# The end of a decoder step: the last output tile's first 256 columns in two products with sums of their own

## The chip, the cores and the metric

The program runs on one core of one Trainium2 chip, as one launch. The metric is device time in microseconds (us). Before the change three runs gave 953.62, 954.85 and 957.12 us; the median is 954.85 us.

## The reference, cut to what matters

One trunk layer of a decoder for 512 prompt tokens and 8 x 8 sample tokens, 1024 channels wide, all in float32. The change lies in its last two operations: the down-projection of the feed-forward part with its gated residual add, and the final RMSNorm.

```python
def _rmsnorm(x, g):
    x32 = x.astype(jnp.float32)
    y = x32 * lax.rsqrt(jnp.mean(x32 * x32, axis=-1, keepdims=True) + RMS_EPS)
    return (y * g.astype(jnp.float32)).astype(x.dtype)
...
    x = x + g2 * ((jax.nn.gelu(ac, approximate=False) * val) @ w_down)
...
    y_prompt = _rmsnorm(xp, final_g)
    y_sample = _rmsnorm(xs, final_g)
```

Every token's output needs the mean of the squares of all its 1024 channels, so no row of a token can be written before the last channel tile of that token is known.

## The kernel before, in words

Activations lie transposed: channels on the 128 partitions, tokens along the free axis. `x1` is a list of NK = 8 channel tiles of 128 x 576: columns 0 to 511 are the prompt tokens, columns 512 to 575 the sample tokens. `GRP = [(0, 256), (256, 576)]` cuts the columns into group 0 and group 1. At the very end the columns are seen as token tiles of 128 (`tok_cols`, L891): tile 0 is columns 0 to 127, tile 1 columns 128 to 255, tiles 2 and 3 the rest of the prompt, and tile 4 columns 448 to 575, of which only the 64 sample tokens are used.

A float32 product is made of three products of a faster form: each operand is split into a high and a low part (`fh`, `fl` for activations, `wh`, `wl` for weights), and high x high, low x high and high x low are added up in PSUM. The down-projection has 22 contraction tiles. Tiles 16 to 21 are the last stretch, and there the channel tiles 6 and 7 (`LATE = 2`) are made last, plainly: for a channel tile and a column group, 6 contraction tiles x 3 products = 18 matmuls into one PSUM bank (`down_late`, L2303, by `product_g`, L231). The weight part is the stationary operand, the activations move.

After such a product come, in this order:

- `residual` (L1640): VectorE reads PSUM, multiplies with the gate and adds to `x1[m]`.
- `summed` (L2211): ScalarE squares the result into `sq`; VectorE adds it to the sum of squares `acc3`, except for the very last piece, whose `sq` is kept apart; then ScalarE multiplies `x1[m]` in place with the gains of the final norm.
- `final_rows` (L2223): TensorE adds up squares over the channels, by a matmul with a 128 x 2 tile of ones (`acc3`, and for the last piece `sq` too), so that each token of a tile gets its sum on its own partition. `rows_rsqrt` (L624) scales it on VectorE and raises it to the power -1/2 on GpSimd, into a column of `r3`.
- `TokenTile` (L1809): `turn` transposes the eight channel tiles of one token tile by TensorE into two PSUM banks (a matmul with `ident`); `finish` reads both banks, multiplies each row with its factor in `r3` and writes `yo`, one bank by ScalarE and one by VectorE, and starts a store of each half.

PSUM has two pools here: `mmps()` gives one of two 128 x 1024 tiles (two banks each), `aux()` one of four banks.

Before the change the end runs so. Product of tile 6, group 0. Product of tile 7, group 0, of which four of six contraction tiles are made, 12 matmuls; then, between them (`between`), the row factors of tiles 2, 3 and 4 and the transposes and stores of tiles 2 and 3; then the other 6 matmuls. Then tile 4, then the row factors of tiles 0 and 1 in one go, then tiles 0 and 1. In tile 4, VectorE reads one bank and ScalarE the other. Stores go out on SyncE's queue, but for the two of tile 1, which ScalarE issues.

From `pinned.extend([pe, act, dve])` (L2313) on, the instructions of TensorE, ScalarE and VectorE stay in the order in which the program writes them. Each engine takes its own in that order, so an instruction that waits holds up all that are written behind it on its engine.

Of the kernel before, what the change touches and what calls it, by code (L numbers as in the profile page):

```python
# [12 lines left out]
AF = mybir.ActivationFunctionType  # L13
ALU = mybir.AluOpType
AX = mybir.AxisListType

P = 128
D = 1024
NK = D // P
# [3 lines left out]
GRP = [(0, 256), (256, 576)]  # L23
# [8 lines left out]
LATE = 2  # L32
# [44 lines left out]
def step_kernel(ctx: ExitStack, tc: tile.TileContext, ins: dict, outs: list):  # L77
    nc = tc.nc
# [14 lines left out]
    def nm(s):  # L93
        cnt[0] += 1
        return f"{s}{cnt[0]}"
# [37 lines left out]
    def sv(t):  # L133
        return t[:, 512:576]
# [474 lines left out]
    ones = cp.tile([P, 2], F32, tag="ones", name="ones")  # L609
# [302 lines left out]
    for i in (3, 4):  # L912
        a = aux()
# [24 lines left out]
    def queries(t, ps=None, scale=HD**-0.5):  # L938
# [50 lines left out]
        out=sel,  # L989
        in0=snk.rearrange("p (h g) -> p h g", h=4),  # L990
# [247 lines left out]
    def b10(t):  # L1238
        return t[:, 514:594].rearrange("p (b e) -> p b e", b=8)
# [184 lines left out]
    ya, w_next, raw_ao, o, late = [], {}, {}, [], []  # L1424
# [56 lines left out]
    for at, m in enumerate(PLAIN):  # L1481
        if at in (4, 5):
            src, dst = ((ins["cache_k_win"], nks), (ins["cache_v_win"], nvs))[at - 4]
# [39 lines left out]
        if at == len(PLAIN) - 1:  # L1523
# [5 lines left out]
        ps = product(w, h, steps)  # L1529
# [3 lines left out]
            out=b10(u)[:, :, 2:10], in0=b8(sv(ps)), in1=b8(sv(c_sb)), op=ALU.mult  # L1533
# [67 lines left out]
    for n, m in enumerate(turn):  # L1601
# [6 lines left out]
        ps = product(w_next.pop(n), o)  # L1608
# [31 lines left out]
    def residual(ps, xt, blk, c0=0, c1=NT, tail=dve):  # L1640

        p1 = min(c1, 512)
        dve.scalar_tensor_tensor(
            out=xt[:, c0:p1], in0=ps[:, : p1 - c0], scalar=modT[:, blk, 0:1], in1=xt[:, c0:p1],
            op0=ALU.mult, op1=ALU.add,
        )
        if c1 > 512:
            t = sp.tile([P, 64], F32, tag="rt", name=nm("rt"))
            tail.tensor_tensor(
                out=b8(t), in0=b8(ps[:, p1 - c0 :]), in1=bc(modT[:, blk, 1:9]), op=ALU.mult  # L1650
            )
            tail.tensor_tensor(out=sv(xt), in0=sv(xt), in1=t, op=ALU.add)
# [19 lines left out]
    x1 = [x1t[k // 4][:, k % 4, :] for k in range(NK)]  # L1672
# [20 lines left out]
    late = []  # L1693
# [115 lines left out]
    class TokenTile:  # L1809
# [14 lines left out]
        def finish(self, queues):  # L1824
            r, i = self.rows, self.i
            out = [slot("yo", shape=[P, 512]) for _ in range(2)]
            fr = r3[r, i : i + 1]
            a, d = (1, 0) if i == 4 else (0, 1)
            act.activation(out[a][r], self.ps[a][r], AF.Copy, scale=fr)
            dve.tensor_scalar(  # L1830
                out=out[d][r], in0=self.ps[d][r], scalar1=fr, scalar2=None, op0=ALU.mult
            )
            for hh, queue in enumerate(queues):
                cs = slice(hh * 512, hh * 512 + 512)
                dst = y_p[0, i * P : i * P + P, cs] if i < 4 else y_s.flatten_outer_dims()[:, cs]
                queue.dma_start(dst, out[hh][r])
# [309 lines left out]
    for k0, m in CHUNKS.items():  # L2146
        r = lambda *x, k0=k0: raw_op(k0, *x)
# [31 lines left out]
    for n, at in enumerate(order):  # L2179
# [7 lines left out]
        if n + 2 < len(order):  # L2187
            kind, m = order[n + 2]
# [7 lines left out]
        else:  # L2196
            summed = n + 1 in prepared
# [10 lines left out]
    acc3 = slot("acc")  # L2208
    r3 = cp.tile([P, 8], F32, tag="r3", name="r3")

    def summed(m, c0=0, c1=NT, last=False):  # L2211

        sq = acc3 if m == 0 else slot("sq")
        act.activation(sq[:, c0:c1], x1[m][:, c0:c1], AF.Square)
        if m and not last:
            dve.tensor_tensor(
                out=acc3[:, c0:c1], in0=acc3[:, c0:c1], in1=sq[:, c0:c1], op=ALU.add
            )
        x = x1[m][:, c0:c1]
        act.activation(x, x, AF.Copy, scale=par2T[:, 66 + m : 67 + m])  # L2220
        return sq

    def final_rows(g, sq=None):  # L2223

        a = mmps()
        i0, i1, step = (0, 2, 512) if g == 0 else (2, 5, 2)
        parts = [acc3] if sq is None else [acc3, sq]
        for n, x in enumerate(parts):
            for i in range(i0, i1):
                dst = a[:, (i - i0) * step : (i - i0) * step + 2]  # L2230
                matmul(dst, tok_cols(x, i), ones, start=n == 0, stop=n == len(parts) - 1)
        src = a[:, : (i1 - i0) * step].rearrange("p (i e) -> p i e", e=step)[:, :, 0]
        rows_rsqrt(r3[:, i0:i1], src)

    late, jobs, weight_steps = [], {}, {}
# [39 lines left out]
    fa = [fs.pop(m) for m in range(PLAIN_AT, LAST_AT)]  # L2275
# [24 lines left out]
        summed(m)  # L2300
    fa = [fs[m] for m in range(LAST_AT, NF)]

    def down_late(m, g, between=None):  # L2303
        ps = product_g(late[m - NK + LATE], fa, g, None if (m, g) == (NK - 1, 1) else mmps(), between)
        residual(ps, x1[m], 40 + m, *GRP[g])
        return summed(m, *GRP[g], last=(m, g) == (NK - 1, 0))

    for m in range(NK - LATE, NK):
        down_late(m, 1)
    down_late(NK - LATE, 0)  # L2310
    for m in range(NK - LATE + 1, NK - 1):
        down_late(m, 0)
    pinned.extend([pe, act, dve])  # L2313

    def others():
        final_rows(1)
        for i in (2, 3):
            tt = TokenTile(i)
# [12 lines left out]


_TC = {"schedule_with_timeline_sim": True}
# [31 lines left out]
```

## Time and profile before

| what | value |
|---|---|
| median of three runs | 954.85 us |
| the profiled execution's own time | 955.27 us |
| its span, first to last instruction | 953.5 us |
| mean granted TensorE clock | 0.996 |
| TensorE busy (matmul records) | 936.5 us, 98% of the span |
| VectorE, ScalarE, GpSimd busy | 739.7, 600.5, 199.8 us |
| last matmul record ends | about 946.3 us into the span |

The profiled execution's own time is 1.77 us longer than its span. A row of the timeline gives the start in the span, the time from the first start to the last end of the merged instructions, the engine, the source line, the operation, output and input by the program's names, the shape and the count; in brackets the idle time before it and who ended it. `PE` is TensorE, `PEld` its weight loads, `DVE` VectorE, `ACT` ScalarE, `POOL` GpSimd, `SPq` and `ACTq` the issue of DMAs by SyncE and ScalarE. Most operations here go through one recording helper, so all of them carry line 116 and are told apart by the names of their tiles.

### The profile page before, as it was taken

Reading aid. Unit: us, or ns where it says so; the run is one execution under the profiler, and the core shown is the slowest. Engines: PE = TensorE matmul, PEld = TensorE weight load, DVE = VectorE, ACT = ScalarE, POOL = GpSimd, SP = SyncE. Lnnn points to the kernel's source line nnn. Section 1 sums busy time; section 2 is a strip of 40 time slices with the busy share of each in tenths; the row PEclk is TensorE's granted clock in tenths of the full one; section 3 lists DMA queues with packets and bytes.
Section 4 is the critical chain, followed back from the end, with each engine's and each line's share of the span. In section 5 each row is a group of like instructions: output and inputs, shape, how many; then the busy total and the mean of one; then the engine's idle time right before and its main releaser. Section 6 shows DMA issues by size and latency. Waiting matters only on the chain. (4 is left out here: it accounts for less than half of the span.)

```text
span 953.5 us, 19148 instructions
## 1 busy us (share of the span) xinstructions
PE 936.5 (98%) x7227; PEld 901.4 (95%) x7227; DVE 739.7 (78%) x1395; ACT 600.5 (63%) x1158; POOL 199.8 (21%) x426
## 2 busy tenths in 40 slices
PE   7999999999999999999999999999999999999996
PEld 5799999898999989999889999999999999999996
DVE  4788988875866767876677688888888889877965
ACT  5474768656665446875335567577766776677574
POOL 2222120101111011210001231122243233421131
PEclk9999999999999999999999999999999999999998
DMA  9984233516545768899884832368679877986643
GB/s 281 329 252 109 70 101 98 157 70 151 141 130 171 248 217 214 213 248 291 278 289 122 184 102 67 96 137 198 164 153 233 207 169 167 228 211 151 143 97 105
DMA packets 190032, 166.74 MB, mean 175 GB/s; under 512 B 9177, under 2 KB 162973, under 8 KB 189651
## 3 DMA queue, kind: packets, MB, share of 16 engines
q1 hardware_dynamic: 172210, 114.41, 40.3%
q0 software_dynamic: 17440, 50.58, 24.8%
q8 instruction: 57, 0.93, 0.4%
q10 hardware_dynamic: 288, 0.52, 0.1%
q14 instruction: 37, 0.30, 0.1%
HBM read 116.84 MB, written 15.02 MB: 138 GB/s over the span
## 5 line engine op out<-in xcount | busy, mean ns | idle before, releaser
L116 ACT ACTIVATE whi<-raw 128x1024 fp32r<-128x1024 f32 (+3 forms) x198 | 195.4, 996 | 35.7 <-DVE raw L116 18.0
L116 DVE TENSOR_TENSOR wlo<-raw,whi 128x1024 fp32r<-128x1024 f32 (+3 forms) x153 | 176.1, 1156 | 33.9 <-ACT whi L116 33.4
L116 POOL DMA_DIRECT2D wlo<-raw x45 | 39.0, 866 | 207.2 <-PE mm L116 96.2
L116 DVE TENSOR_TENSOR raw<-raw 128x512 f32<-128x512 f32 (+1 forms) x104 | 69.2, 665 | 3.4
L116 PE MATMUL aux<-2h,whi 128*128 128x288 f32 (+2 forms) x232 | 63.5, 294 | 0.0
L116 PE MATMUL aux<-2l,whi 128*128 128x288 f32 (+2 forms) x232 | 63.5, 295 | 0.0
L116 PE MATMUL mm<-hh,whi 128*128 128x256 f32 (+2 forms) x264 | 60.4, 304 | 0.5 <-ACT hh L116 0.5
L116 PE MATMUL mm<-hl,whi 128*128 128x256 f32 (+2 forms) x264 | 57.3, 297 | 0.0
L116 PE MATMUL mm<-hh,wlo 128*128 128x256 f32 (+2 forms) x264 | 55.4, 295 | 0.0
L116 PE MATMUL aux<-hl,whi 128*128 128x288 f32 (+1 forms) x196 | 53.3, 298 | 0.0
L116 PE MATMUL aux<-hh,whi 128*128 128x288 f32 (+1 forms) x196 | 53.2, 297 | 0.0
L116 POOL DMA_DIRECT2D wl<-s x41 | 35.6, 867 | 71.4 <-ACT wl L116 53.6
L116 ACT ACTIVATE mm<-aux 128x288 f32<-128x288 f32 x49 | 19.5, 397 | 46.7 <-PE aux L116 46.6
L116 ACT ACTIVATE wlo<-whi 128x1024 fp32r<-128x1024 f32 (+1 forms) x45 | 45.4, 1009 | 0.4
L116 PEld LDWEIGHTS mm<-hh,whi 128*128 128x128 f32 x264 | 43.8, 189 | 1.5 <-ACT hh L116 1.0
L116 PEld LDWEIGHTS mm<-hl,whi 128*128 128x128 f32 x264 | 44.1, 188 | 0.9 <-DVE hl L116 0.9
L116 PEld LDWEIGHTS aux<-2l,whi 128*128 128x128 f32 x232 | 43.6, 188 | 0.0
L116 PEld LDWEIGHTS mm<-hh,wlo 128*128 128x128 f32 x264 | 43.6, 188 | 0.0
L116 PEld LDWEIGHTS aux<-2h,whi 128*128 128x128 f32 x232 | 43.5, 188 | 0.0
L116 PE MATMUL aux<-2h,wlo 128*128 128x288 f32 (+2 forms) x232 | 42.1, 295 | 0.0
L1034 ACT ACTIVATE s<-s,nmx 128x256 f32<-128x256 f32 (+1 forms) x72 | 34.0, 477 | 9.6 <-DVE nmx L1028 8.9
L116 ACT ACTIVATE aux<-mm 128x288 f32<-128x288 f32 x52 | 20.6, 396 | 30.6 <-PE mm L116 29.5
(420 smaller groups left out, 3119.2 us busy)
## 6 DMA issues: line engine op xcount, KB each, us to landing
raw<-in_w_in SPq DMA_DIRECT2D x52, 512.0 KB, 4.8
raw<-in_w_up SPq DMA_DIRECT2D x44, 512.0 KB, 4.1
wlo<-raw POOLq DMA_DIRECT2D x34, 512.0 KB, 4.8
ada<-in_w_ada SPq DMA_DIRECT2D x64, 256.0 KB, 5.4
raw<-in_w_down SPq DMA_DIRECT2D x44, 192.0 KB, 3.4
ad<-in_w_ada SPq DMA_DIRECT2D x32, 256.0 KB, 6.2
wl<-s POOLq DMA_DIRECT2D x30, 256.0 KB, 4.3
sg_dram<-sg POOLq DMA_DIRECT2D x16, 288.0 KB, 4.3
```

Source lines behind the costliest of these rows:

```text
L116: done = getattr(self.engine, name)(*args, **kwargs)
L1034: nc.scalar.activation(s[x // 2][:, x % 2, :w], s[x // 2][:, x % 2, :w], AF.Exp, bias=nmx[:, x : x + 1], accum_out=den[:, x : x + 1],)
```

## The change: what it does

The first 256 columns of channel tile 7 are no longer one product but two, of 128 columns each, for token tile 1 and then for token tile 0 (`down_last`). Each has its own 18 matmuls, its own residual add, its own squares and its own row factors. Row factors of tiles 2 to 4 now take the last squares of tile 7's group 1 by TensorE from `sq`, instead of after an addition on VectorE. Tile 4 is read by ScalarE alone, both halves. The order at the end becomes: product for tile 1; row factors of tiles 2 to 4; row factor of tile 1; tile 2; product for tile 0; tile 3; transposes of tile 4; row factor of tile 0; tile 4's reads; tile 1; tile 0. All stores go out on SyncE's queue but one, the first half of tile 0, which ScalarE issues.

```diff
@@ TokenTile.finish
-            a, d = (1, 0) if i == 4 else (0, 1)
-            act.activation(out[a][r], self.ps[a][r], AF.Copy, scale=fr)
-            dve.tensor_scalar(
-                out=out[d][r], in0=self.ps[d][r], scalar1=fr, scalar2=None, op0=ALU.mult
-            )
+            act.activation(out[0][r], self.ps[0][r], AF.Copy, scale=fr)
+            if i == 4:
+                act.activation(out[1][r], self.ps[1][r], AF.Copy, scale=fr)
+            else:
+                dve.tensor_scalar(
+                    out=out[1][r], in0=self.ps[1][r], scalar1=fr, scalar2=None, op0=ALU.mult
+                )
@@ final_rows
-    def final_rows(g, sq=None):
+    def final_rows(i0, i1, sq):
 
         a = mmps()
-        i0, i1, step = (0, 2, 512) if g == 0 else (2, 5, 2)
-        parts = [acc3] if sq is None else [acc3, sq]
-        for n, x in enumerate(parts):
-            for i in range(i0, i1):
-                dst = a[:, (i - i0) * step : (i - i0) * step + 2]
-                matmul(dst, tok_cols(x, i), ones, start=n == 0, stop=n == len(parts) - 1)
+        for i in range(i0, i1):
+            for n, x in enumerate((acc3, sq)):
+                dst = a[:, 2 * (i - i0) : 2 * (i - i0) + 2]
+                matmul(dst, tok_cols(x, i), ones, start=n == 0, stop=n == 1)
@@ the end
+    def down_last(i):
+
+        (hi, lo), c0, c1 = late[-1], i * P, i * P + P
+        ps = mmps()[:, :P]
+        for k, (xh, xl) in enumerate(fa):
+            for n, (wt, x) in enumerate(((hi(k), xh), (hi(k), xl), (lo(k), xh))):
+                matmul(ps, wt, x[:, c0:c1], start=k + n == 0, stop=(k, n) == (len(fa) - 1, 2))
+        residual(ps, x1[NK - 1], 40 + NK - 1, c0, c1)
+        return summed(NK - 1, c0, c1, last=True)
+
-    for m in range(NK - LATE, NK):
+    for m in range(NK - LATE, NK - 1):
         down_late(m, 1)
-    down_late(NK - LATE, 0)
-    for m in range(NK - LATE + 1, NK - 1):
+    sq = down_late(NK - 1, 1, True)
+    for m in range(NK - LATE, NK - 1):
         down_late(m, 0)
     pinned.extend([pe, act, dve])
-
-    def others():
-        final_rows(1)
-        for i in (2, 3):
-            tt = TokenTile(i)
-            tt.turn(range(NK))
-            tt.finish((nc.sync, nc.sync))
-
-    sq = down_late(NK - 1, 0, (3, others))
-    tt = TokenTile(4)
-    tt.turn(range(NK))
-    tt.finish((nc.sync, nc.sync))
-    final_rows(0, sq)
-    for i, last in ((0, nc.sync), (1, nc.scalar)):
-        tt = TokenTile(i)
-        tt.turn(range(NK))
-        tt.finish((last, last))
+    sq1 = down_last(1)
+    final_rows(2, 5, sq)
+    final_rows(1, 2, sq1)
+    out = TokenTile(2)
+    out.turn(range(NK))
+    out.finish((nc.sync, nc.sync))
+    sq0 = down_last(0)
+    out = TokenTile(3)
+    out.turn(range(NK))
+    out.finish((nc.sync, nc.sync))
+    out = TokenTile(4)
+    out.turn(range(NK))
+    final_rows(0, 1, sq0)
+    out.finish((nc.sync, nc.sync))
+    for i, queues in ((1, (nc.sync, nc.sync)), (0, (nc.scalar, nc.sync))):
+        out = TokenTile(i)
+        out.turn(range(NK))
+        out.finish(queues)
```

Up to the product of tile 6, group 0, the order of the instructions on all five engines is the same in both programs. In the rows below, `mm` and `aux` are PSUM tiles, `x_6532` the channel tiles 0 to 3 of `x1` and `x_6533` the tiles 4 to 7, `acc` and `sq` sums and squares, `r` the row factors. First TensorE, before: the last of the first 12 matmuls of tile 7's product, what stands between, and the first of the other 6.

```order
L116 MATMUL mm_12053<-fh_11294,wl_11890 128x256
L116 MATMUL mm_12066<-ones,acc_11299 128x2 x3
L116 MATMUL aux_12072<-ident,x_6532 128x128 x4
L116 MATMUL aux_12073<-ident,x_6533 128x128 x4
L116 MATMUL aux_12088<-ident,x_6532 128x128 x4
L116 MATMUL aux_12089<-ident,x_6533 128x128 x4
L116 MATMUL mm_12053<-fh_11388,wh_11893 128x256
```

The same place after the change, from the row sums of token tile 4 (the last of three such pairs) over those of tile 1 and the transposes of tile 2 to the first matmul of the product for tile 0.

```order
L116 MATMUL mm_12075<-ones,acc_11299 128x2
L116 MATMUL mm_12075<-ones,sq_12025 128x2
L116 MATMUL mm_12084<-ones,acc_11299 128x2
L116 MATMUL mm_12084<-ones,sq_12072 128x2
L116 MATMUL aux_12089<-ident,x_6532 128x128 x4
L116 MATMUL aux_12090<-ident,x_6533 128x128 x4
L116 MATMUL mm_12105<-fh_11093,wh_11889 128x128
```

A whole 18-matmul product for tile 1 now stands ahead of the row sums, where 12 of 18 stood; the row sums have eight matmuls instead of three; and 18 matmuls of tile 0's product stand ahead of the transposes of tile 3.

TensorE's last rows before the change: tile 4, the row sums of tiles 0 and 1, tiles 0 and 1.

```order
L116 MATMUL mm_12114<-ident,x_6532 128x128 x4
L116 MATMUL mm_12114<-ident,x_6533 128x128 x4
L116 MATMUL mm_12129<-ones,acc_11299 128x2 x2
L116 MATMUL mm_12129<-ones,sq_12111 128x2 x2
L116 MATMUL aux_12136<-ident,x_6532 128x128 x4
L116 MATMUL aux_12137<-ident,x_6533 128x128 x4
L116 MATMUL aux_12152<-ident,x_6532 128x128 x4
L116 MATMUL aux_12153<-ident,x_6533 128x128 x4
```

And after it, from the transposes of tile 3 on: tile 4, the row sum of tile 0, tiles 1 and 0.

```order
L116 MATMUL aux_12128<-ident,x_6532 128x128 x4
L116 MATMUL aux_12129<-ident,x_6533 128x128 x4
L116 MATMUL mm_12144<-ident,x_6532 128x128 x4
L116 MATMUL mm_12144<-ident,x_6533 128x128 x4
L116 MATMUL mm_12153<-ones,acc_11299 128x2
L116 MATMUL mm_12153<-ones,sq_12125 128x2
L116 MATMUL aux_12164<-ident,x_6532 128x128 x4
L116 MATMUL aux_12165<-ident,x_6533 128x128 x4
L116 MATMUL aux_12180<-ident,x_6532 128x128 x4
L116 MATMUL aux_12181<-ident,x_6533 128x128 x4
```

Tile 3 has moved behind the last product, and tile 1 stands ahead of tile 0.

VectorE's end before the change, from its last two additions of squares.

```order
L116 TENSOR_TENSOR acc_11299<-acc_11299,sq_12025 128x320
L116 TENSOR_TENSOR acc_11299<-acc_11299,sq_12049 128x256
L116 TENSOR_SCALAR r_11300<-mm_12066 128x3
L116 TENSOR_SCALAR yo_12083<-aux_12073,r_11300 128x512
L116 TENSOR_SCALAR yo_12099<-aux_12089,r_11300 128x512
L116 SCALAR_TENSOR_TENSOR x_6533<-mm_12053,modT,x_6533 128x256
L116 TENSOR_SCALAR yo_12123<-mm_12114,r_11300 64x512
L116 TENSOR_SCALAR r_11300<-mm_12129 128x2
```

The same stretch after the change.

```order
L116 TENSOR_TENSOR acc_11299<-acc_11299,sq_12048 128x256
L116 SCALAR_TENSOR_TENSOR x_6533<-mm_12052,modT,x_6533 128x128
L116 TENSOR_SCALAR r_11300<-mm_12075 128x3
L116 TENSOR_SCALAR r_11300<-mm_12084 128x1
L116 TENSOR_SCALAR yo_12100<-aux_12090,r_11300 128x512
L116 SCALAR_TENSOR_TENSOR x_6533<-mm_12105,modT,x_6533 128x128
L116 TENSOR_SCALAR yo_12139<-aux_12129,r_11300 128x512
L116 TENSOR_SCALAR r_11300<-mm_12153 128x1
```

One addition of 128 x 320 is gone, the read of tile 4 (`64x512`) no longer stands ahead of the last row factor, and there are three row-factor steps instead of two.

More of the change, by code (lines that the diff above doesn't have):

```diff
@@ L2221, in summed @@
         return sq
-    def final_rows(g, sq=None):
+    def final_rows(i0, i1, sq):
         a = mmps()
-        i0, i1, step = (0, 2, 512) if g == 0 else (2, 5, 2)
-        parts = [acc3] if sq is None else [acc3, sq]
-        for n, x in enumerate(parts):
-            for i in range(i0, i1):
-                dst = a[:, (i - i0) * step : (i - i0) * step + 2]
-                matmul(dst, tok_cols(x, i), ones, start=n == 0, stop=n == len(parts) - 1)
-        src = a[:, : (i1 - i0) * step].rearrange("p (i e) -> p i e", e=step)[:, :, 0]
+        for i in range(i0, i1):
+            for n, x in enumerate((acc3, sq)):
+                dst = a[:, 2 * (i - i0) : 2 * (i - i0) + 2]
+                matmul(dst, tok_cols(x, i), ones, start=n == 0, stop=n == 1)
+        src = a[:, : 2 * (i1 - i0)].rearrange("p (i e) -> p i e", e=2)[:, :, 0]
         rows_rsqrt(r3[:, i0:i1], src)
@@ L2301, in step_kernel, with down_late @@
     fa = [fs[m] for m in range(LAST_AT, NF)]
-    def down_late(m, g, between=None):
-        ps = product_g(late[m - NK + LATE], fa, g, None if (m, g) == (NK - 1, 1) else mmps(), between)
+    def down_late(m, g, last=False):
+        ps = product_g(late[m - NK + LATE], fa, g, aux() if last else mmps())
         residual(ps, x1[m], 40 + m, *GRP[g])
-        return summed(m, *GRP[g], last=(m, g) == (NK - 1, 0))
-    for m in range(NK - LATE, NK):
+        return summed(m, *GRP[g], last=last)
+    def down_last(i):
[7 more added lines that the diff above has]
+    for m in range(NK - LATE, NK - 1):
         down_late(m, 1)
-    down_late(NK - LATE, 0)
-    for m in range(NK - LATE + 1, NK - 1):
+    sq = down_late(NK - 1, 1, True)
+    for m in range(NK - LATE, NK - 1):
         down_late(m, 0)
     pinned.extend([pe, act, dve])
-    def others():
-        final_rows(1)
-        for i in (2, 3):
-            tt = TokenTile(i)
-            tt.turn(range(NK))
-            tt.finish((nc.sync, nc.sync))
-    sq = down_late(NK - 1, 0, (3, others))
-    tt = TokenTile(4)
-    tt.turn(range(NK))
-    tt.finish((nc.sync, nc.sync))
-    final_rows(0, sq)
-    for i, last in ((0, nc.sync), (1, nc.scalar)):
-        tt = TokenTile(i)
-        tt.turn(range(NK))
-        tt.finish((last, last))
+    sq1 = down_last(1)
[16 more added lines that the diff above has]
+        out.finish(queues)
 _TC = {"schedule_with_timeline_sim": True}
```

## The prediction

> **What bounds the kernel now.** I began with the page's first part, to see which engine carries the span.
>
> ```profile
> span 953.5 us, 19148 instructions
> PE 936.5 (98%) x7227; PEld 901.4 (95%) x7227; DVE 739.7 (78%) x1395; ACT 600.5 (63%) x1158; POOL 199.8 (21%) x426
> ```
>
> TensorE has something in flight for 98% of the span. Up to the product of tile 6, group 0, no engine's order changes, so only the last stretch counts. There I read the chain of waits, from 939 us on.
>
> ```profile
> 938.98 0.51 DVE acc L116
> ...
> 940.39 0.17 DVE r L116
> 940.57 0.07 issue
> 940.64 0.88 POOL r L116
> 941.52 4.61 issue
> 946.12 0.74 POOLq L2361
> ```
>
> The end hangs on GpSimd's power step for the row factors of tiles 0 and 1, which ends at 946.9. The 4.61 us of "issue" ahead of it are what the view cannot name; the timeline of all engines over the same stretch does.
>
> ```profile
> 942.72 1.04 PE L116 MATMUL mm<-ident,x 128*128 128x128 f32 x8
> ...
> 943.59 0.51 PE L116 MATMUL mm<-ones,acc 128*128 128x2 f32 x4
> ...
> 943.95 0.59 PE L116 MATMUL mm<-ones,sq 128*128 128x2 f32 x4
> ...
> 944.40 1.94 PE L116 MATMUL aux<-ident,x 128*128 128x128 f32 x16
> 944.41 0.68 ACT L116 ACTIVATE yo<-mm,r 64x512 f32<-64x512 f32 x1
> 945.13 0.76 DVE L116 TENSOR_SCALAR yo<-mm,r 64x512 f32<-64x512 f32 x1 [1.73 <-ACT yo L116]
> 945.92 0.16 DVE L116 TENSOR_SCALAR r<-mm 128x2 f32<-128x2 f32 x1
> 946.16 0.69 POOL L116 TENSOR_TENSOR r<-r,mhalf 128x2 f32<-128x2 f32 x1 [4.64 <-DVE r L116]
> 946.89 1.26 ACT L116 ACTIVATE yo<-aux,r 128x512 f32<-128x512 f32 x2 [1.79 <-POOL r L116]
> 946.89 1.41 DVE L116 TENSOR_SCALAR yo<-aux,r 128x512 f32<-128x512 f32 x2 [0.81 <-POOL r L116]
> 948.18 0.88 ACTq L1836 DMA_DIRECT2D out<-yo  x2
> ```
>
> The row sums of tiles 0 and 1 are there at 943.95 + 0.59 = 944.54, but VectorE scales them at 945.92. Ahead of that step stands its read of tile 4, which waits until ScalarE has read the other bank, and then takes 0.76 us. This costs 945.92 - 944.54 = 1.4 us. TensorE itself is done at 944.40 + 1.94 = 946.34 and waits for nothing any more. From 946.89 come two reads on each of two engines (to 948.30) and the last stores. The transfers are seen in the DMA view of 942 to 954, 40 slices of 0.3 us, and in the windows view.
>
> ```profile
> GB/s 0 0 0 75 396 376 389 382 383 410 376 410 273 14 212 171 137 198 171 27 27 178 375 389 396 355 389 369 396 375 260 7 20 14 0 0 0 0 0 0
> ...
> out<-yo SPq DMA_DIRECT2D x6, 256.0 KB, 2.4
> out<-yo ACTq DMA_DIRECT2D x2, 256.0 KB, 3.6
> out<-yo SPq DMA_DIRECT2D x2, 128.0 KB
> ```
> ```profile
> 948.40:951.40 3.00, 0.00 (x0) 0.00 (x0) 0.00 (x0) 0.00 (x0) 0.00 (x0) 0.54 0.94 348
> 951.40:953.50 2.10, 0.00 (x0) 0.00 (x0) 0.00 (x0) 0.00 (x0) 0.00 (x0) 0.50 0.02 6
> ```
>
> The last four stores of 256 KB (1.05 MB) run at about 385 GB/s, 2.7 us, and end in the slice at 951.0, at 951.2 by its share. Behind them lie some 2.3 us in which nothing but the close runs, and the profiled execution's 1.77 us outside the span. I leave both as they are. The profiled execution took 955.27 us, 0.42 more than the median of 954.85; what the sum adds to it I add to the median.
>
> **The change part by part.** *The product in halves.* Before, it is one product of 256 columns; its step from matmul to matmul and those of 128 columns are read from TensorE's timeline at two places: at the end, and in the attention scores, where a moving operand in the same split form is 128 wide.
>
> ```profile
> 937.67 0.28 PE L116 MATMUL mm<-fh,wl 128*128 128x256 f32 x1
> 937.79 0.28 PE L116 MATMUL mm<-fh,wh 128*128 128x256 f32 x1
> ...
> 939.09 0.28 PE L116 MATMUL mm<-fh,wl 128*128 128x256 f32 x1
> ```
> ```profile
> 81.58 0.28 PE L116 MATMUL aux<-kh,q 128*128 128x128 f32 x1
> ...
> 82.14 0.27 PE L116 MATMUL aux<-kl,q 128*128 128x128 f32 x1
> 82.25 0.35 PE L116 MATMUL mm<-hh,whi 128*128 128x256 f32 x1
> ```
>
> From 937.79 to 939.09 are 11 steps: 0.118 us each. From 81.58 to 82.25 are six: 0.112 us. So half the columns cost 95% of the time: two halves are 36 x 0.112 = 4.03 us where 18 x 0.118 = 2.12 stood, +1.91 us on TensorE. What a short matmul waits for is, by these rows, not its columns.
>
> The Trainium skill, TensorE: Matmul & The Clock Gate, section Back-to-back issue gap, gives about 81 ns a matmul for a sustained stream at 128 columns. By it the halves would take an estimated 2.9 us; the trace's 128-wide rows, at 112 ns, do not bear that out.
>
> *Row sums.* Plain float32 matmuls show twice in the trace: the two with `acc` and the two with `sq` at 943.59 and 943.95 are four records each, and from 943.95 to 944.40 four take 0.45 us, 0.1125 each. Now there are 6 + 2 + 2 matmuls, 20 records, 2.25 us; before there were 3 + 4, 14 records, 1.58 us: +0.67. In return VectorE's addition of 128 x 320 (0.51 us in the chain) and TensorE's wait for it go.
>
> *TensorE's new end.* A transpose steps by (943.59 - 942.72) / 8 = 0.109, a token tile takes 0.87 us. From 937.79 on I lay the pieces one behind the other:
>
> - product for tile 1: 2.02, to 939.81
> - 16 records of row sums for tiles 2 to 4 and 1: 1.80, to 941.61
> - tile 2: 0.87, to 942.48
> - product for tile 0: 2.02, to 944.49
> - tile 3: 0.87, to 945.36; tile 4: 0.87, to 946.24
> - row sums of tile 0: 0.45, to 946.69
> - tiles 1 and 0: 1.74, to 948.43, the last record ending at 948.60 (1.04 - 0.87 = 0.17 later).
>
> That needs waits that stay covered. Row sums of tile 1 need the product's residual add and squares: for 128 columns neither is in this stretch, so the bounds are other operations of that width and the same ones at 256.
>
> ```profile
> L1160 DVE SCALAR_TENSOR_TENSOR s<-V,aux 128x128 f32<-128x128 f32 x16 | 3.7, 284 | 1.5 <-PE aux L116 1.4
> ...
> L116 DVE SCALAR_TENSOR_TENSOR x<-mm,modT,x 128x256 f32<-128x256 f32 x2 | 1.0, 484 | 0.5 <-PE mm L116 0.5
> ...
> L1202 ACT COPY ot<-aux 128x128 f32<-128x128 f32 x32 | 6.0, 270 | 6.7 <-PE aux L1191 6.7
> ...
> L116 ACT ACTIVATE sq<-x 128x256 f32<-128x256 f32 x5 | 2.1, 412 | 2.6 <-DVE x L116 2.6
> ```
>
> The product's last record ends at 939.81 - 0.11 + 0.28 = 939.98. With 0.28 to 0.48 for the add, 0.27 to 0.41 for the squares and some 0.15 between the engines they are there at 940.7 to 941.0; TensorE asks at 939.81 + 14 x 0.1125 = 941.39. Covered, by 0.4 us at least; I take nothing. Behind that matmul the whole rest of TensorE would wait. For tile 0 the cover is tiles 3 and 4, 1.7 us.
>
> *Row factors.* Tiles 2 to 4: sums at 941.30, VectorE 0.16, GpSimd 0.88, with the 0.25 and 0.03 between them of the chain above: 942.5. Tile 2 is transposed at 942.65, so this is covered by 0.15 us. Tile 0: sums at 946.83, a power step of one column, not shown, is at most the 0.69 of two, so ready by 947.9; tile 0's first bank is transposed at 948.17. Covered. Tile 4 on ScalarE alone takes 0.76 us off VectorE ahead of that factor and puts a second 0.68 on ScalarE. ScalarE reads tile 4 from 946.45 in two steps of 0.58, then tile 1, and comes to tile 0 at 948.2, when its bank is there. The 1.4 us wait is gone, but TensorE is late instead: tile 0's second bank is read from 948.64 to 948.64 + 0.75 = 949.39, where the reads ended at 948.30: +1.09. The last store is issued at 949.4; before, at 948.18 + 0.88 / 2 = 948.6. That is +0.8.
>
> *Stores.* Tile 3 no longer goes out at 943 but behind the product for tile 0: read from 945.57, first store at 946.35. SyncE's queue takes nine of ten stores instead of eight. From issue to data lie, before, 942.26 to about 943.14, 0.88 us:
>
> ```profile
> 942.26 6.15 SPq L1836 DMA_DIRECT2D out<-yo  x8
> ```
>
> So from 947.23 on run tile 3, tile 4, tile 1, tile 0: six of 256 KB and two of 128 KB, 1.84 MB. At 385 GB/s they take 4.77 us and end at 952.0: +0.8. Tile 4's two stores, alone on the queue, ran at 137 to 212 GB/s, 0.75 us each instead of 0.34. If they keep that, the end is 952.8: +1.6. Then each went out alone, behind reads that ended 0.8 us apart (945.09 and 945.89); now they stand in a full queue, so I lean to the fast end.
>
> *Sum:* issue path +0.8, store path +0.8 to +1.6: I take +1.0. 955.27 + 1.0 = 956.3 for the profiled execution, **955.8 us** for the median.
>
> **The rivals.** *Short matmuls run faster (not slower than before).* The four records from 943.59 to 943.95 stepped by 0.09 us at most, so 0.112 may not be the floor. At 0.09 the pieces ahead of tile 3, 36 matmuls and 16 sums, are 1.15 us shorter; first and last stores move up by that: +0.8 - 1.15 = -0.3, 954.5 us. For it speaks that step; against it the six steps of 0.112 in the same form and width. It decides as soon as a step is under 0.097. Chance 0.20. By the 81 ns of the Trainium skill (the page and section above) the estimate is 36 x 0.031 = 1.1 us less, the same time.
>
> *Tile 4's stores keep their slow pace behind tile 3's:* +1.6, 956.5 us. For it speaks the GB/s row from 946.2 to 947.7; against it that there the queue was empty between the two. It decides once the eight stores together take over 5 us. 0.15.
>
> *Short products fall back to the plain form (slower than before by more than can be mistaken).* The row sums show that a plain float32 matmul is two records. If a product 128 columns wide were run so too, 36 more records of 0.112 come, all ahead of tile 0: +1.0 + 4.0, 959.9 us. The attention rows speak against it: one record each. 0.03.
>
> *The change does not do what it says:* a row factor is still held up by a read. By the order above it could only be tile 0's, whose cover is 0.3 us; the price is at most the 0.76 of one read, inside the range.
>
> **How the numbers follow.** The forecast, +0.6 to +1.3, has 0.55; the rivals 0.20, 0.15 and 0.03; 0.07 is for what I do not see, in either direction. A measurement of this kernel tells some 0.5%, 4.8 us, from no change; all but the plain form lie within it. So faster 0.01, same 0.95, slower 0.04. The range holds -0.3 and +1.6, 954.5 to 956.5, and about half of the spread that the three runs show around their median (-1.2, +2.3): 953.9 to 957.6.
>
> **What would show it.** In the changed profile: 18 records per half, stepping by 0.112; no idle on TensorE from 937.8 on; its last record at 948.6; GpSimd's last power step done before tile 0 is transposed; VectorE's last read at 949.4; DMA without a gap from tile 3's first store to the end. The forecast is wrong if TensorE ends before 948, if it waits for squares, or if the GB/s row has a gap ahead of the last stores.

## The result and the profile after

The changed kernel took 958.27 us in the median of ten runs (955.74 to 963.51), the kernel before 954.39 us in ten runs beside it. The ratio is 1.0041, with an interval of 1.0027 to 1.0055. The change makes the kernel slower, by 3.9 us where 0.95 was forecast, and the time lies above the range. The profiled run happens to be the quickest of the ten, 955.74 us; that has to be kept in mind all through this section.

First the page's first part, after:

```profile
span 954.0 us, 19198 instructions
PE 938.9 (98%) x7251; PEld 902.9 (95%) x7251; DVE 739.1 (77%) x1395; ACT 601.9 (63%) x1161; POOL 200.7 (21%) x427
```

Then the chain of waits, from 935 us on; its columns are start, duration, and the work or wait:

```profile
935.86 5.81 PE mm L116 x52
941.67 0.93 PE aux L116 x8
942.60 1.96 PE mm L116 x18
944.57 0.90 PE aux L116 x8
945.46 1.22 PE mm L116 x12
946.67 1.82 PE aux L116 x16
948.49 0.04 DVEq L116
948.53 0.05 issue
948.58 0.75 DVE yo L116
```

Where GpSimd's power step and 4.61 us of "issue" stood before, there is TensorE from end to end. The wait that the change was to remove is gone. The timeline of the same stretch gives each piece:

```profile
937.82 0.22 PE L116 MATMUL mm<-fh,wh 128*128 128x128 f32 x1
...
939.78 0.33 PE L116 MATMUL mm<-ones,acc 128*128 128x2 f32 x2
...
941.53 1.07 PE L116 MATMUL aux<-ident,x 128*128 128x128 f32 x8
942.36 0.30 PE L116 MATMUL mm<-fh,wh 128*128 128x128 f32 x1
...
944.40 1.06 PE L116 MATMUL aux<-ident,x 128*128 128x128 f32 x8
945.30 1.04 PE L116 MATMUL mm<-ident,x 128*128 128x128 f32 x8
...
946.54 1.94 PE L116 MATMUL aux<-ident,x 128*128 128x128 f32 x16
```
```profile
946.71 0.16 DVE L116 TENSOR_SCALAR r<-mm 128x1 f32<-128x1 f32 x1 [0.46 <-PE mm L116]
946.95 0.55 POOL L116 TENSOR_TENSOR r<-r,mhalf 128x1 f32<-128x1 f32 x1 [4.04 <-DVE r L116]
...
947.72 1.61 DVE L116 TENSOR_SCALAR yo<-aux,r 128x512 f32<-128x512 f32 x2 [0.84 <-PE aux L116]
```

In this execution TensorE's part of the tail is what the prediction laid out: 18 steps from 937.82 to 939.78 and from 942.36 to 944.40, the last record at 946.54 + 1.94 = 948.48, the last read at 947.72 + 1.61 = 949.33. The GB/s row of 942 to 954.5, 40 slices of 0.31 us, shows the eight stores without a gap:

```profile
GB/s 0 0 0 0 0 0 229 360 380 446 262 0 7 7 13 26 242 374 374 400 321 236 197 210 164 295 400 400 400 393 387 393 393 295 0 0 0 0 0 0
```

They start in the slice at 947.0 and end at 952.5. The four slices of 164 to 236 are tile 4's. The span grew by 0.5 us only. The windows view adds the granted TensorE clock, as a share of full speed; its columns are the stretch and its length, busy time and instructions of PE, PEld, DVE, ACT and POOL, then the granted clock, the DMA share and GB/s. The tail kept the full clock:

```profile
936.00:940.00 4.00, 4.00 (x38) 4.00 (x37) 2.78 (x8) 3.79 (x8) 0.00 (x0) 1.00 0.00 0
940.00:944.00 4.00, 4.00 (x38) 4.00 (x38) 1.40 (x4) 1.40 (x3) 1.41 (x2) 1.00 0.00 1
944.00:948.00 4.00, 4.00 (x40) 4.00 (x39) 1.54 (x4) 2.89 (x6) 0.55 (x1) 1.00 0.59 219
```

So the profile after explains nothing of the 2.5 us by which the median lies over this one run. Another profile of the same kernel shows what lies behind it.

### The profile page after: what moved, and what is told of

It reads as the page before. It is cut to its first block, busy times and chain, and to the rows that moved or that the text cites. A ratio compares the mean times of both kernels' runs of the same rounds, so it can differ in the third digit from the quotient of the medians.

```text
span 954.0 us, 19198 instructions
## 1 busy us (share of the span) xinstructions
PE 938.9 (98%) x7251; PEld 902.9 (95%) x7251; DVE 739.1 (77%) x1395; ACT 601.9 (63%) x1161; POOL 200.7 (21%) x427
```

## Experiments

Each kernel was run beside the kernel before on the same chip. The ratio and its 95% interval are those on record; they are not the quotient of the two medians, and where the two disagree the difference is not clear of the noise.

### The same kernel again

> The changed kernel again, for its scatter and a second profile. The sum of the tail: the profiled end moves by +0.5 to +1.0 us and no more, every execution within 1 us of 955.7. Scatter theory (the tail costs under 1 us, and some 3 us more come from places ahead of the tail or from waits that vary between executions): executions from 955.5 to 962, median near 958, and a slow execution's profile shows a TensorE gap that the quick one lacks, with a lower mean clock (the spans of the ten executions so far go with the mean clock: 954.0 at 0.998, 961.7 at 0.993).

958.64 us in the median of 6 runs, before 954.93; ratio 1.0042 [1.0029, 1.0055]. The profiled run took 957.77 us, the quickest of the six, 0.9 us under their median. Its windows:

```profile
936.00:940.75 4.75, 4.75 (x45) 4.75 (x44) 2.40 (x7) 3.45 (x9) 0.32 (x1) 1.00 0.00 0
940.75:941.00 0.25, 0.25 (x5) 0.25 (x3) 0.05 (x1) 0.00 (x0) 0.25 (x1) 0.73 0.00 0
941.00:947.50 6.50, 6.50 (x32) 6.50 (x32) 1.10 (x2) 1.95 (x4) 0.84 (x2) 0.50 0.22 83
947.50:947.75 0.25, 0.25 (x4) 0.25 (x3) 0.20 (x1) 0.03 (x1) 0.00 (x0) 0.62 0.00 0
947.75:950.00 2.25, 2.25 (x23) 2.25 (x22) 0.80 (x3) 1.40 (x3) 0.55 (x1) 1.00 0.36 137
```

The granted clock drops to 0.50 inside the tail; I call such a stretch a fall. A slice at 0.73 has 0.23 / 0.50 of its 0.25 us at full clock, so the fall begins at 940.75 + 0.115 = 940.87; by the slice at 0.62 it ends at 947.69. It lasts 6.82 us. TensorE is busy in every slice: no wait lies in it. Its timeline shows what that does to the steps:

```profile
936.75 0.22 PE L116 MATMUL mm<-fh,wh 128*128 128x128 f32 x1
...
940.46 1.59 PE L116 MATMUL aux<-ident,x 128*128 128x128 f32 x8
941.70 0.46 PE L116 MATMUL mm<-fh,wh 128*128 128x128 f32 x1
...
945.59 1.93 PE L116 MATMUL aux<-ident,x 128*128 128x128 f32 x8
...
948.74 1.94 PE L116 MATMUL aux<-ident,x 128*128 128x128 f32 x16
```

The second product takes 945.59 - 941.70 = 3.89 us where 2.04 stood. From the first narrow matmul to the last 16 transposes are 11.99 us, against 946.54 - 937.82 = 8.72 in the profile above: +3.27 us, about half of 6.82. That is about the size of the miss, 3.9 - 0.95 = 2.95 us. The two profiled times differ by 2.03 us only, mainly because this tail begins 1.07 us earlier.

The kernel before kept the full clock in its profiled tail:

```profile
936.00:940.00 4.00, 3.84 (x34) 3.64 (x32) 3.19 (x8) 3.75 (x8) 0.00 (x0) 1.00 0.00 0
940.00:944.00 4.00, 4.00 (x39) 4.00 (x38) 2.01 (x4) 1.80 (x4) 0.88 (x1) 1.00 0.22 83
944.00:946.00 2.00, 2.00 (x20) 2.00 (x21) 0.84 (x2) 1.07 (x2) 0.00 (x0) 1.00 0.95 355
```

One profile doesn't tell how often the clock falls, but every execution has a mean granted clock on record. It averages 0.9954 over the 16 executions of the changed kernel and 0.9977 over the 29 of the kernel before: an estimate of 0.0023 x 957 = 2.2 us more lost to the clock per execution. A single mean says little, since it holds the idle end and the start of the program too; the profile before, at 0.996 in all, has its half-clock stretch at 17 to 20 us. What follows: the changed kernel's time is its sum plus a fall of the clock in many of its executions; the run of 955.74 us is one without. This isn't all of the scatter: an execution of 958.07 us had a mean clock of 0.998, like that of 955.74, and what made it late, or those of 961.59 and 963.51 us so late, is not shown. What lets the clock fall was still to be found.

### Which part of the change costs the time

Tile 4 read by ScalarE alone, the rest as before:

```diff
-            a, d = (1, 0) if i == 4 else (0, 1)
-            act.activation(out[a][r], self.ps[a][r], AF.Copy, scale=fr)
+            act.activation(out[0][r], self.ps[0][r], AF.Copy, scale=fr)
+            if i == 4:
+                act.activation(out[1][r], self.ps[1][r], AF.Copy, scale=fr)
+            else:
...
```

> The kernel before with one part of the change: tile 4 read by ScalarE alone. Nothing else moves. By the chain of before the last row factor starts 1.2 us earlier and the last reads end some 0.7 to 1.0 us earlier: -0.7 us, about 953.7. Scatter theory: executions as tight as before, since TensorE's program is the same. If the median rises by over 2 us, this part carries the loss.

954.15 us against 954.93; ratio 1.0001 [0.999, 1.0012], 12 runs. Its profile has the last reads done at 946.37, against 948.30 before, but its tail also begins 0.76 us earlier, and the median doesn't tell it from the kernel before. A gain of the expected size is not shown; this part is no loss.

The change with one product of 256 columns for tiles 0 and 1:

```diff
-    sq1 = down_last(1)
+    sq0 = down_late(NK - 1, 0, True)
     final_rows(2, 5, sq)
-    final_rows(1, 2, sq1)
...
-    sq0 = down_last(0)
...
-    final_rows(0, 1, sq0)
+    final_rows(0, 2, sq0)
```

> The changed kernel with the halves undone: one product of 256 columns, one pair of row sums for tiles 0 and 1, the rest as changed. The tail sum: TensorE has 36 x 0.112 - 18 x 0.118 = 1.9 us less, so it ends near 946.7; the stores of tile 3 start some 1.9 us earlier than in the changed kernel; -0.5 to -1.0 us against before, about 953.7. If the scatter hangs on the second product, executions are as tight as before; if it hangs on the order of the stores or on ScalarE's share, the median stays near 957 to 958.

955.49 us against 954.93; ratio 1.0002 [0.9992, 1.0012], 11 runs. So the loss goes when the halves go; the row sums of tile 1 that stood between them go with them, and the runs further down part the two.

The kernel before with 24 matmuls at TensorE's very end that nothing reads:

```diff
+    spare = mmps()
+    for n in range(24):
+        matmul(spare[:, 0:128], late[-1][0](n % 4), fa[n % 4][0][:, 0:128], start=n == 0, stop=n == 23)
```

> The kernel before with 24 more matmuls of 128 columns at the end of TensorE's program, for which nothing waits (extra work whose result goes nowhere). They run from 946.4 to 949.1, beside the last stores. Tail theory (the loss comes from who waits for whom in the tail): no change, within 0.5 us of before. Program theory (a longer TensorE program, with more of its code fetched while the stores run, is what scatters): executions from 955 to 962 like the changed kernel, +2 to +4 us.

955.05 us; ratio 1.0006 [0.9996, 1.0016], 11 runs. More instructions for TensorE as such cost nothing that can be told, at most 1.5 us by the interval. That theory falls.

### Wider products in the same places

The changed kernel, both products streaming all 256 columns, of which only the 128 of their own are read: as many matmuls in the same order, twice the columns.

```diff
-        ps = mmps()[:, :P]
+        ps = mmps()[:, : 2 * P]
...
-                matmul(ps, wt, x[:, c0:c1], start=k + n == 0, stop=(k, n) == (len(fa) - 1, 2))
-        residual(ps, x1[NK - 1], 40 + NK - 1, c0, c1)
+                matmul(ps, wt, x[:, : 2 * P], start=k + n == 0, stop=(k, n) == (len(fa) - 1, 2))
+        residual(ps[:, c0:c1], x1[NK - 1], 40 + NK - 1, c0, c1)
```

> The changed kernel, but each of the two last products streams all 256 columns and only its own 128 are read: the same number of matmuls in the same order, more work in the array. Clock theory (in a stretch of short products, row sums and transposes the array works too little, the granted clock falls to 0.50 for a window of some 3.4 or 6.8 us, and when that window falls inside the tail the matmuls step by 0.213 instead of 0.112): steps of 0.118, +0.2 us by the sum, but no or rare drops of the clock ahead of 945 us, executions from 954 to 957, median about 955.8, nearly 3 us quicker than the changed kernel. Rival (the tail's order, the row sums or the stores make the scatter): like the changed kernel or slower, median 958.5 to 959, and from 956 to 963.

955.94 us against 954.62; ratio 1.0012 [1.0000, 1.0024], 12 runs. More work in the same order is 2.4 us quicker than the changed kernel, each counted from its own kernel before (1.32 against 958.64 - 954.93 = 3.71). Ten of the 12 runs lie at 956.92 us or less; the other two, 958.59 and 960.12 us, had the lowest mean clocks, 0.996, and no profile. The profiled run keeps the clock:

```profile
936.00:948.00 12.00, 12.00 (x108) 12.00 (x108) 5.53 (x16) 7.78 (x17) 1.97 (x3) 1.00 0.18 65
```

The kernel before, with its last product alone made as 36 matmuls of 128 columns, both halves in turn, in the old order:

```diff
+                    for c in (0, P):
+                        matmul(
+                            ps[:, 4 * c : 4 * c + P], wt, x[:, c : c + P],
+                            start=k + n == 0, stop=(k, n) == (len(fa) - 1, 2),
+                        )
...
```

> The kernel before with nothing changed but the shape of the last product: 36 matmuls of 128 columns instead of 18 of 256, both halves in turn, one residual add, one row factor step, everything else in its old order. Sum at full clock: +1.9 us on TensorE, 24 of the 36 ahead of tiles 2 and 3: about 956.8. Clock theory: on top of that drops of the clock in the tail in part of the executions, median 957.5 to 959, executions up to 962. Rival: 956.8 and as tight as before.

957.25 us against 954.62; ratio 1.0019 [1.0009, 1.0028], 9 runs; no fall in the profile. Narrow matmuls in the old order cost 2.6 us, somewhat more than their sum of 1.9. So not all of the loss needs the new order; the fall of the clock, as far as one profile tells, needs the narrow products and the new order together.

A third order, with the whole product and no halves:

```diff
...
+    sq = down_late(NK - 1, 0)
+    final_rows(1)
+    token_tile(2, (nc.sync, nc.sync))
+    final_rows(0, sq)
+    for i in (3, 4, 1):
+        token_tile(i, (nc.sync, nc.sync))
+    token_tile(0, (nc.scalar, nc.sync))
```

> A version that draws on the runs so far: tile 4 read by ScalarE alone, the last product whole (256 columns) ahead of all row sums, row sums of tiles 0 and 1 right behind the transposes of tile 2, then tiles 3, 4, 1, 0. TensorE as long as before; the stores run from 943.6 without a gap and end near 949.7 where they ended at 951.2 before: -1.1 us against before, 953.8, if the clock holds. Clock theory: behind the last wide matmul stand 6 us of row sums and transposes, so a drop of the clock is as likely as in the run with the whole product, and it doubles the steps of some transposes: part of the executions 2 to 3 us later.

954.25 us against 954.62; ratio 0.9997 [0.9989, 1.0006], 11 runs. No fall, and no gain that can be told either; where the expected gain went was not settled.

### Which of the two products, or the row sums

The changed kernel with tile 7's last squares added by VectorE as before, so that TensorE has 10 records of row sums between the products instead of 16:

```diff
+        parts = (acc3,) if sq is None else (acc3, sq)
...
-        return summed(m, *GRP[g], last=last)
+        return summed(m, *GRP[g], last=False)
...
-    final_rows(2, 5, sq)
+    final_rows(2, 5, None)
```

> The changed kernel, but the row sums of tiles 2 to 4 come from the sum of squares alone: VectorE adds tile 7's last squares as before the change, and TensorE has 10 records of row sums between the two products instead of 16. Theory A (the clock falls because of the stretch of 128 x 2 row sums between the narrow products): falls become rarer, a median of 955.5 to 956.5 us, at least 1.5 us under the changed kernel. Theory B (the narrow width of the products alone lets the clock fall): falls as often as in the changed kernel; shorter by 6 x 0.1125 = 0.7 us, less some 0.5 us of waiting for VectorE's addition: 957.5 to 958.5 us.

956.17 us against 955.38; ratio 1.0013 [0.9999, 1.0026]. The falls are rarer, as theory A had it. The 12 runs fall apart: eight from 954.29 to 956.58, four from 958.63 to 959.83. Three of the four had a mean clock of 0.993, the fourth 0.997, within what the eight had, so a fall as long as the one below is not in it. One of the three was profiled:

```profile
939.75:940.00 0.25, 0.25 (x4) 0.25 (x3) 0.16 (x1) 0.00 (x1) 0.25 (x1) 0.65 0.00 0
940.00:950.00 10.00, 10.00 (x50) 10.00 (x49) 2.01 (x4) 3.23 (x6) 1.41 (x3) 0.50 0.28 107
950.00:950.25 0.25, 0.25 (x4) 0.25 (x3) 0.00 (x0) 0.00 (x0) 0.03 (x1) 0.87 0.00 0
```

Here the fall lasts from 939.83 to 950.07, 10.24 us.

The changed kernel with only the first product streaming 256 columns, of which 128 are read; for the second product alone, the condition is `i == 0`:

```diff
+        w0, w1 = (0, 2 * P) if i == 1 else (c0, c1)
+        ps = mmps()[:, : w1 - w0]
...
```

> The changed kernel, but the product for token tile 1, ahead of the row sums, streams all 256 columns, of which the 128 of its own are read; the product for tile 0 stays narrow. By the steps alone 18 x 0.006 = +0.1 us against the changed kernel. If the fall is decided by the width of the products taken together: falls in part of the runs, 956.5 to 957.5 us. If it is the first product (the falls were seen to begin at its end): none, 955.5 to 956.5 us. If it is the second: as the changed kernel, 958 to 959 us.

955.26 us against 955.38; ratio 1.0004 [0.9995, 1.0013], 11 runs, the clock at 1.00 throughout the profiled tail. (The fall of the second profile began at 940.87, 2.2 us behind the end of the first product at 938.71, and not at that end, as I had put it.)

> The changed kernel, but the product for token tile 0, behind the row sums, streams all 256 columns, of which the 128 of its own are read; the product for tile 1 stays narrow. By the steps alone 18 x 0.006 = +0.1 us against the changed kernel. If the first product decides the fall: falls as in the changed kernel, and the second product then takes 18 x 0.235 instead of 18 x 0.213: 958 to 959 us. If the second one decides: none, 955.5 to 956.5 us. If both together: 956.5 to 957.5 us.

956.73 us; ratio 1.0015 [1.0005, 1.0026], 11 runs. Its profile has a short fall:

```profile
942.25:942.50 0.25, 0.25 (x5) 0.25 (x3) 0.00 (x0) 0.00 (x0) 0.25 (x1) 0.80 0.00 0
942.50:945.75 3.25, 3.25 (x17) 3.25 (x16) 0.75 (x1) 0.69 (x1) 0.62 (x2) 0.50 0.42 161
945.75:946.00 0.25, 0.25 (x4) 0.25 (x4) 0.00 (x0) 0.00 (x0) 0.00 (x0) 0.87 0.00 0
```

From 942.40 to 945.82: 3.42 us. The row sums and both products carry weight, the first product most: where it is wide, the time is that of the kernel before.

### The rule that the profiles bear out

The three falls last 3.42, 6.82 and 10.24 us: one, two and three times 3.41. And in all three the next drop, when TensorE has ended, lies on the same grid (in the second profile of the changed kernel at 954.51, 6.82 behind the rise at 947.69). The Trainium skill, TensorE: Matmul & The Clock Gate, section What's actually happening, says that activity is watched in windows of 3413 ns that run freely and don't begin with the kernel, and that the idle state is half rate; the trace agrees in length and in the halves, and the drop behind the end gives the grid of each profile.

With the grid, each stretch of a profile can be filled from its timeline with the time that TensorE spent on wide products, narrow products, row sums and transposes (us), and set against the clock that followed it:

| profile, stretch ending at | wide | narrow | row sums | transposes | work as weighted below | clock behind it |
|---|---|---|---|---|---|---|
| changed, second profile, 940.87 | 0 | 1.25 | 1.75 | 0.41 | 1.36 | 0.50 |
| fewer row sums, 939.83 | 0.05 | 1.95 | 1.20 | 0.21 | 1.44 | 0.50 |
| second product wide, 942.40 | 0 | 0.99 | 1.76 | 0.66 | 1.49 | 0.50 |
| tile 4 alone, 947.58 (then idle) | 0 | 0 | 0 | 1.41 | 1.41 | 0.50 |
| changed, first profile, 940.46 | 0.77 | 1.96 | 0.68 | 0 | 1.85 | 1.00 |
| changed, first profile, 943.87 | 0 | 1.51 | 1.07 | 0.83 | 1.77 | 1.00 |
| first product wide, 941.67 | 0.40 | 0.48 | 1.70 | 0.83 | 1.80 | 1.00 |
| halves whole again, 943.24 | 0 | 0 | 1.16 | 2.25 | 2.48 | 1.00 |

One set of weights orders all of them: wide products and transposes counted whole, narrow products at 0.48, row sums at 0.2, and the clock halved where a stretch sums to less than some 1.5 to 1.77 us, half of 3.41 being 1.71. The weights are fitted to these rows, so they are an estimate. By them, with the limit at 1.71, the changed kernel falls at 88% of the places that the grid can have, with the second product wide at 58%, with fewer row sums at 33%, with the first product wide at 18%. That is the order of their medians over the kernel before: +3.7, +1.35, +0.8 and -0.1 us. These shares hang on the limit: at 1.5 they would be some 42, 42, 11 and 0%. The kernel before with its last product narrow would fall at some 22%; its one profile has no fall. With both products wide, or one whole product, it falls nowhere. Both wide doesn't fit into that order: +1.3 us without a fall, as much as the sum of its tail. Why the other forms hide that sum, and this one not, stays open; it is within the microsecond by which the start of the tail scatters (936.75 and 937.82 in the two profiles of the changed kernel).

What these windows count, that section of the Trainium skill doesn't say beyond how busy TensorE has been, and it gives the half rate to idle windows; here TensorE was in flight in every slice and the clock fell all the same. The same page of the Trainium skill, section Part 4: PE-mode transpose, says that transposes don't count as busy in the same way. Here 2.25 us of them with 1.16 us of row sums kept the full clock: the measurement decides, and in this kernel they count.

Two kernels tested the rule, with numbers written ahead. The first has fewer row sums and both products narrow, in an order that puts transposes between the sums:

```diff
     final_rows(2, 5, None)
-    final_rows(1, 2, sq1)
     out = TokenTile(2)
...
-    sq0 = down_last(0)
+    final_rows(1, 2, sq1)
     out = TokenTile(3)
...
+    sq0 = down_last(0)
     out = TokenTile(4)
```

> The kernel with fewer row sums between the products, in another order: row sums of tiles 2 to 4, tile 2, row sum of tile 1, tile 3, product for tile 0, tile 4. The same instructions, both products narrow. Theory A (in each stretch of 3.41 us on a fixed grid TensorE's work is added up, transposes and 256-wide matmuls counted whole, 128-wide ones at about half, row sums at about 0.2, and under some 1.7 us the clock is halved for the next stretch): the lowest stretch at any place of the grid has 1.72 to 1.89 us, so no fall or next to none: median 0 to 0.8 us over the kernel before, no run with the two long rows of a fall. Theory B (narrow products alone lower the clock, whatever stands between): falls as often as with fewer row sums, 4 of 12 runs 3 us late, and a median 0.8 to 1.5 us over the kernel before.

954.79 us against 954.80; ratio 1.0001 [0.9991, 1.0011]; 11 of 12 runs at 955.94 or less. The clock of its profiled tail:

```profile
936.00:946.00 10.00, 10.00 (x93) 10.00 (x93) 4.90 (x12) 6.62 (x15) 1.98 (x3) 1.00 0.28 105
```

The same instructions as with fewer row sums in another order, and one late run (958.29) where four of 12 were; its mean clock was 0.999, the highest of the 12, so it was not late by the clock.

The second is the kernel before, all products wide, with 18 more row sums that nothing reads:

```diff
+        if g == 1:
+            for n in range(18):
+                matmul(a[:, 512 + 2 * n : 514 + 2 * n], tok_cols(acc3, 2 + n % 3), ones, start=True, stop=True)
```

> The kernel before, its products 256 wide, with 18 idle row sums of the sum of squares (36 records of 0.1125 = 4.05 us) behind those of tiles 2 to 4; nothing reads them. Theory A (little array work in a stretch of 3.41 us halves the clock, whatever the width of the products): the stretch of row sums is 4.72 us long, so at any place of the grid one stretch has at most 1.0 us of work: a fall in every run, seen in the profile as 0.50 behind the row sums for one or two stretches, which costs 1.7 to 3.4 us beside the 4.05: 5.8 to 7.5 us over the kernel before. Theory B (the narrow products are needed): no fall, 4.05 us over the kernel before.

964.20 us against 954.80, 6 runs, ratio 1.0093 [1.0078, 1.0108]: +9.4 us, more than either theory gave. All six have mean clocks of 0.991 to 0.994. The windows and the timeline of its profile:

```profile
941.25:941.50 0.25, 0.25 (x4) 0.25 (x3) 0.00 (x0) 0.00 (x0) 0.00 (x0) 0.73 0.00 0
941.50:951.50 10.00, 10.00 (x48) 10.00 (x49) 1.67 (x3) 1.38 (x2) 0.88 (x1) 0.50 0.17 65
951.50:951.75 0.25, 0.25 (x4) 0.25 (x3) 0.00 (x0) 0.00 (x0) 0.00 (x0) 0.79 1.07 418
```
```profile
939.49 7.44 PE L116 MATMUL mm<-ones,acc 128*128 128x2 f32 x42 [0.16 <-DVE acc L116]
946.79 3.65 PE L116 MATMUL aux<-ident,x 128*128 128x128 f32 x16
```

The fall came, with no narrow product in the kernel, and lasted from 941.37 to 951.61, 10.24 us: three stretches where I had allowed two. 4.05 + 10.24 / 2 = 9.2 us, close to the 9.4 measured. Runs of row sums bring the clock down without any narrow product. What I had wrong is both ends of the fall. The stretch ahead of it holds 1.38 us of wide products and 1.87 us of row sums, which weigh 1.75 us: more than half of 3.41, and the clock fell. With the first profile's 1.77, which kept it, that leaves 1.75 to 1.77 us as the limit by these weights, and with them it holds for every stretch at full clock in the tails of all 14 profiles. On the way back, of the stretches at half clock in the four falls, those weighted at 0.7 to 2.55 us stayed low, and those at 2.73 and more were followed by the full clock: by these weights, coming back takes more than staying at full clock does. What exactly is counted stays open.

## Why the prediction was wrong, by its own steps

- **TensorE's end, reads and waits: right at full clock.** Record end 948.48 for 948.60, last read 949.33 for 949.39; no wait for squares, the power step done at 947.50, ahead of tile 0. Only the read of tile 2's first bank waited for its factors, until 942.42, and TensorE did not wait for it.
- **The step that failed is "two halves are 36 x 0.112 = 4.03 us", with the pieces laid behind one another in it.** Each duration was right and each was taken at the full clock for good. 0.112 holds only while the clock does; in the second profile the second half stepped by 3.89 / 18 = 0.216. No term and no rival had the clock, though the same page of the Trainium skill that I drew on for the short matmuls states the windows of 3413 ns. Read by its words alone, idle and busy windows, it would not have given a fall where TensorE is busy in every slice; that the work in a window counts, and not its busy time, only the runs showed.
- **The premise behind that step**, never written down, is that a TensorE that is busy without a gap keeps its clock. A row sum of 2 columns and a matmul of 128 columns fill the busy column as well as one of 256; in the second profile the busy share was full and the clock 0.50.
- **Short matmuls faster than 0.112:** no; 0.109 to 0.114 at full clock in the profiles, never under the 0.097 that was to decide it.
- **Tile 4's stores slow:** this rival's sign came: the eight stores took 952.5 - 947.0 = 5.5 us, over its 5. Tile 4's ran at 164 to 236 GB/s in a full queue too. The data end 1.3 us later than before, between the +0.8 that I leaned to and the rival's +1.6.
- **"Some 2.3 us of close ... left as they are":** not so; 954.0 - 952.5 = 1.5 us. So the span grew by 0.5 us, half of the +1.0 of the sum, though the data end came 0.5 us later than 952.0: two errors that cancel in part, by luck. Why the close is shorter was not tried.
- **Sign and size:** slower was forecast and came, but through a fall of the clock that no term held. A rival that ends slower by more was there, the plain form, with the wrong mechanism. The right one could have been priced: the profile before shows the clock at 0.50 from 18 to 20 us, so the price of a fall, half its length, was at hand. With the two stretches of the second profile, known only afterwards, it gives +3.4 us, 959.2 us.

## What to carry to other kernels

Before work on TensorE is cut into smaller matmuls or gathered into runs of tiny ones, add up what TensorE does in any 3.4 us of it, by width and not by busy time. In this kernel, runs of row sums, alone or with narrow matmuls, halved the clock for the work behind them; transposes or wide products between them, or streaming wider than is needed, kept it. One profile, above all one whose time is far from the median, may not hold what sets the median: read the granted clock by stretches in a run near it.

## What the runs showed of the hardware

- The granted clock halved while TensorE was busy in every slice: for 3.42, 6.82 and 10.24 us, on a grid of 3.41 us that lies differently in each execution.
- Streaming columns that nobody reads made the changed kernel 2.4 us quicker; 36 more records of row sums made the kernel before 9.4 us slower, of which their own time is 4.05.
- Stores of 128 KB from 64 partitions moved at 164 to 236 GB/s with other stores queued ahead and behind, those of 256 KB from 128 partitions at 360 to 446 in the full slices of the same row.
